# A gated linear recurrence: the factor of its input as (1 + a) times a root of tanh of half the exponent

## The chip, the core and the metric

The kernel runs on one core of one Trainium2 chip. The time is that of the device, in microseconds, from one execution's start to its end; a median is taken over executions of the same kernel. The engines are called by the profile's names: PE is TensorE's matmul, PEld its weight load, DVE is VectorE, ACT is ScalarE, POOL is GpSimd, SP is SyncE (which issues the DMAs).

## What is computed

Two layers over 512 tokens (256 of context, 256 latent) of width 2048. Each layer normalises and modulates its input, multiplies it with a large matrix `w_in`, feeds the columns to three mixers (a bidirectional gated linear recurrence, windowed attention, a bidirectional state-space part of the Mamba-2 kind), and multiplies the mix with `w_out`. The change concerns the recurrence, which runs in both directions over 1024 channels:

```python
r = sigmoid(einsum(xb, w_a) + b_a)             # 16 blocks of 64 x 64
i = sigmoid(einsum(xb, w_x) + b_x)
log_a = -LRU_C * r * softplus(-lam)            # LRU_C = 8
a = exp(log_a)
b = sqrt(-expm1(2.0 * log_a)) * (i * xf)
h = linear_scan(a, b, reverse)                 # h[t] = a[t] * h[t-1] + b[t]
```

The factor sqrt(1 - a^2) is what the two kernels write differently. With L = `log_a` and a = exp(L) both are exact:

- before: 1 - a^2 = -(1 + a^2) tanh(L), so the factor is the root of (1 + a^2) times -tanh(L);
- after: 1 - a = -(1 + a) tanh(L/2), so 1 - a^2 = -(1 + a)^2 tanh(L/2), and the factor is (1 + a) times the root of -tanh(L/2).

## The kernel before

Activations lie with channels on the partitions and tokens along the row (128x512 tiles, columns 0 to 255 context, 256 to 511 latent). The weights stay in float32 and come from HBM in pieces of 128x512, tile `raw`, on SP's DMA queue. Each piece becomes two matmul operands: `hi`, a rounded copy made on ACT (L237), and `lo`, the rest, a subtraction on DVE (L238), with four buffers each (`HB`). For every 128x128 block PE then runs three matmuls (`hi` with the input's `uh` and `ul`, `lo` with `uh`; L174) that add up in a PSUM tile `acc`. In the second layer the column blocks whose context half nobody reads (the recurrence's gate, among others) have 256 columns, not 512.

Around the change, a layer runs 8 blocks m of 128 channels: first the column block of the recurrence's input (`lru_x`), then that of its gate (`lru_g`). Between the weight matmuls PE runs small steps of the recurrence and of the state-space part, which share four PSUM tiles `mx`: for the recurrence the gate products (`mx<-xc,gw` and `mx<-xsw,gw`, for each direction d), for the state-space part steps of the classes State (tile `xw`, state `H`, L1119 to L1132) and Output (`cbm`, `ee`, `ww`, `bc`, L1151 to L1191). `xsw` (L694) is the convolved input `xc` with its two halves of partitions exchanged.

In `lru_x` each direction runs: two Tanh of the gate products on ACT (L712, into tiles `lt` for r and i), Tanh of the exponent into half of `ltl` (L717), Exp in place in `lt` (L718), Square into `la2` (L720), and on DVE (a^2 + 1) times tanh (L721) and (1 + tanh) times `xc` for the input gate (L722). When both directions are through, one Sqrt covers both halves of `ltl` (L724, 128x1024). It needs another table of functions in ACT than Tanh and Exp do, so an `ACT_TABLE_LOAD` stands ahead of it, and one ahead of the next Tanh or Exp. Then POOL multiplies the gated input with the root (L727), DVE scans (L730 forward; L733 and L735 backward in two halves), and POOL adds the directions (L739). `lru_g` (L745 to L750) multiplies this with the gate and stores it; the mix is read again at the layer's end.

What sets the order: PE's order is the program's own, written out by generators that wait for times in PE work by a table. The order on ACT, DVE, POOL and SP is made when the program is built, by a scheduler's own estimate of when each instruction can run; an engine then runs its list strictly in that order. The tile `la2` shares its four buffers with other roles (`xc`, `lgt`, `xw` among them). Line numbers here are those of the kernel before. In the changed kernel the first Tanh stands at L714, the Tanh of the exponent at L719 and Exp at L720; from L724 on the numbers are equal.

Of the kernel before, what the change touches and what calls it, by code (L numbers as in the profile page):

```python
# [10 lines left out]
AF = mybir.ActivationFunctionType  # L11
ALU = mybir.AluOpType
AX = mybir.AxisListType

P = 128
# [124 lines left out]
class Kernel:  # L140
# [526 lines left out]
    def lru_begin(self, l):  # L667
        nc = self.nc
        o = PARAMS["lam"][0]
        ng = self.t([P, 16], "nlam", 1)  # L670
        nc.vector.tensor_scalar(out=ng, in0=self.prm[:, o:o + 16], scalar1=-1.0, scalar2=None, op0=ALU.mult)
        sp = self.softplus(ng, 16, "lsp")
        self.s4 = self.t([P, 16], "s4", 1)
        nc.vector.tensor_scalar(out=self.s4, in0=sp, scalar1=-4.0, scalar2=None, op0=ALU.mult)
        self.gb = self.t([P, 32], "gbh", 1)
        o = PARAMS["gab"][0]
        nc.vector.tensor_scalar(out=self.gb, in0=self.prm[:, o:o + 32], scalar1=0.5, scalar2=None, op0=ALU.mult)
        self.gws = [self.gate_weights(l, 0)]
        self.lruD = self.dram([8, P, 512], "lruD")
# [8 lines left out]
    def lru_x(self, l, m, px):  # L688
        nc = self.nc
        xc = self.t([P, 512], "xc")  # L690
        self.conv(xc, px, lambda tap: self.par("lcw", tap * 8 + m), self.par("lcb", m), 2)
        xs = self.t([P, 512], "xsw")
        for r, o in ((0, 64), (64, 0)):
            nc.scalar.activation(out=xs[r:r + 64], in_=xc[o:o + 64], func=AF.Copy)  # L694
        gw = self.gws.pop(0)
        if m < 7:
            self.gws.append(self.gate_weights(l, m + 1))
        yield self.wait("lx")
        ab = []
        tl = self.t([P, 2, 512], "ltl", 1)  # L700
        for d in range(2):
            if d:
                yield self.wait("lx2")
            th = []
            pg = [self.mx() for _ in range(2)]
            for r, c in ((0, 0), (64, 64), (0, 64), (64, 0)):
                x = xc if r == c else xs
                self.mm(pg[r // 64][c:c + 64], gw[r:r + 64, int(r != c), 2 * d + r // 64], x[r:r + 64], pos=(r, c),
                        side=4)
            for g in range(2):  # L710
                t = self.t([P, 512], f"lt{g}", 2)
                nc.scalar.activation(out=t, in_=pg[g], func=AF.Tanh, scale=0.5,  # L712
                                     bias=self.gb[:, 16 * g + 8 * d + m:16 * g + 8 * d + m + 1])
                th.append(t)  # L714
            tr, ti = th
            s4 = self.s4[:, 8 * d + m:8 * d + m + 1]
            nc.scalar.activation(out=tl[:, d], in_=tr, func=AF.Tanh, scale=s4, bias=s4)  # L717
            nc.scalar.activation(out=tr, in_=tr, func=AF.Exp, scale=s4, bias=s4)  # L718
            a2 = self.t([P, 512], "la2", 1)  # L719
            nc.scalar.activation(out=a2, in_=tr, func=AF.Square)  # L720
            nc.vector.scalar_tensor_tensor(out=tl[:, d], in0=a2, scalar=1.0, in1=tl[:, d], op0=ALU.add, op1=ALU.mult)  # L721
            nc.vector.scalar_tensor_tensor(out=ti, in0=ti, scalar=1.0, in1=xc, op0=ALU.add, op1=ALU.mult)  # L722
            ab.append((tr, ti))
        nc.scalar.activation(out=tl, in_=tl, func=AF.Sqrt, scale=-0.0625, bias=self.eps["s"])  # L724
        hs = []
        for d, (tr, ti) in enumerate(ab):
            nc.gpsimd.tensor_tensor(out=ti, in0=ti, in1=tl[:, d], op=ALU.mult)  # L727
            h = self.t([P, 512], f"lh{d}", 2)
            if d == 0:
                nc.vector.tensor_tensor_scan(out=h, data0=tr, data1=ti, initial=0.0, op0=ALU.mult, op1=ALU.add)  # L730
            else:
                r = lambda x, s: x[:, s:s + 256][:, ::-1]
                nc.vector.tensor_tensor_scan(out=r(h, 0), data0=r(tr, 0), data1=r(ti, 0), initial=0.0, op0=ALU.mult,  # L733
                                             op1=ALU.add)
                nc.vector.tensor_tensor_scan(out=r(h, C), data0=r(tr, C), data1=r(ti, C), initial=h[:, 0:1],  # L735
                                             op0=ALU.mult, op1=ALU.add)
            hs.append(h)
        s = C if l else 0
        nc.gpsimd.tensor_tensor(out=hs[0][:, s:], in0=hs[0][:, s:], in1=hs[1][:, s:], op=ALU.add)  # L739
        self.lru_h[m] = hs[0]  # L740
# [536 lines left out]
```

## Time and profile before

| | |
|---|---|
| median of three runs | 1831.15 us (1829.35 to 1833.1) |
| profiled execution | 1829.47 us, its span 1827.5 us |
| mean granted clock of PE | 0.991 |
| PE busy | 1765.5 us, 97%, 10522 instructions |
| DVE busy | 1407.4 us, 77%, 3117 |
| ACT busy | 973.3 us, 53%, 1798 |
| POOL busy | 214.7 us, 12%, 179 |

The busy share is over the whole span; matmuls are pipelined, so a busy PE isn't PE at its peak. PEclk is the clock that was granted to PE as a share of full speed (1.0 is 2.4 GHz, 0.5 is 1.2 GHz). The two stages in which recurrence and state-space part run among the weight matmuls are 236 to 490 us (layer 0) and 1290 to 1500 us (layer 1); the profile can be asked for each stretch and for each engine's waits in it. In a list of waits an entry "PE mx L174 <- DVE H L1132" says that a matmul of PE into `mx` waited, and that the instruction that released it was DVE's on tile `H`, line 1132.

### The profile page before, as it was taken

How to read it: one execution, taken by the hardware profiler on the slowest of the kernel's cores; microseconds unless marked ns; L12 is line 12 of the kernel's file. 1: busy time of each engine (PE TensorE's matmuls, PEld its weight loads, DVE VectorE, ACT ScalarE, POOL GpSimd, SP SyncE). 2: the span in 40 equal slices, each digit the busy share in tenths (PEclk: the TensorE clock that was granted, in tenths of full speed). 3: DMA queues.
4: the chain of work that ended last, by engine and by line, in shares of the span. 5: the costliest groups of instructions: out<-in, count | busy, mean ns of one | idle time of the engine just before them, and what ended most of it. 6: DMA issues, size and time to landing. Idle time of an engine off the chain costs nothing.

```text
span 1827.5 us, 30170 instructions
## 1 busy us (share of the span) xinstructions
PE 1765.5 (97%) x10522; PEld 1453.4 (80%) x10522; DVE 1407.4 (77%) x3117; ACT 973.3 (53%) x1798; POOL 214.7 (12%) x179
## 2 busy tenths in 40 slices
PE   7999999999999999999999999999989999999999
PEld 4677876667778778887888887888767788999999
DVE  4447769898899778899999536877688785788665
ACT  4324578688523354556232235545688863678443
POOL 0000111111210021211000021010021130121000
PEclk9999999999999999999999999999999999999999
DMA  9982333434675545556766433455243564554655
GB/s 364 389 292 66 124 104 102 122 122 146 220 221 180 179 150 185 178 182 221 238 220 222 158 122 107 133 185 168 96 138 107 179 214 142 182 178 155 217 185 179
DMA packets 186344, 322.99 MB, mean 177 GB/s; under 512 B 19121, under 2 KB 44625, under 8 KB 185553
## 3 DMA queue, kind: packets, MB, share of 16 engines
q1 hardware_dynamic: 186192, 321.09, 54.2%
q8 instruction: 82, 1.34, 0.3%
q14 instruction: 70, 0.57, 0.1%
HBM read 310.38 MB, written 10.63 MB: 176 GB/s over the span
## 4 chain that ended last, share of the span: by engine, by line
PE 72%; DVE 9%; issue 7%; ACT 7%; DMA 3%; POOL 1%; SPq 0%; ACTq 0%; DVEq 0%; POOLq 0%
PE acc L174 55%; PE mx L174 13%; PE ada L174 3%; DVE lo L238 2%; PE mx L170 2%; DMA bc<-acsD 1%; ACT hi L237 1%; DVE ada L380 1%; DVE araw L380 1%; ACT lt L712 1%; DVE lh L730 1%; DMA araw<-in_adaw_dram 1%; DVE xc L466 1%; DVE ee L1165 1%; ACT ww L1167 1%
## 5 line engine op out<-in xcount | busy, mean ns | idle before, releaser
L174 PE MATMUL acc<-u,hi 128*128 128x512 f32 (+1 forms) x4800 | 1277.4, 355 | 3.9 <-ACT u L452 3.1
L174 PEld LDWEIGHTS acc<-u,hi 128*128 128x128 f32 x4800 | 837.1, 190 | 149.0 <-issue 32.6
L174 PE MATMUL acc<-u,lo 128*128 128x512 f32 (+1 forms) x2400 | 842.4, 351 | 6.9 <-DVE lo L238 6.7
L237 ACT ACTIVATE hi<-raw 128x512 fp32r<-128x512 f32 x640 | 397.8, 628 | 544.4 <-PE acc L174 420.8
L238 DVE TENSOR_TENSOR lo<-raw,hi 128x512 fp32r<-128x512 f32 x640 | 457.9, 718 | 184.6 <-ACT hi L237 172.7
L174 PEld LDWEIGHTS acc<-u,lo 128*128 128x128 f32 x2400 | 455.5, 190 | 71.9 <-DVE lo L238 11.7
L380 DVE SCALAR_TENSOR_TENSOR araw<-araw,adac 128x512 f32<-128x512 f32 x256 | 183.2, 716 | 6.9 <-DMA araw<-in_adaw_dram 4.1
L380 DVE SCALAR_TENSOR_TENSOR ada<-araw,adac 128x512 f32<-128x512 f32 x192 | 141.6, 738 | 13.0 <-DMA adac<-condD 7.0
L174 PE MATMUL mx<-u,hi 128*128 128x512 f32 (+1 forms) x320 | 99.7, 395 | 0.0
L1077 DVE SCALAR_TENSOR_TENSOR X<-acc,mod,X 128x256 f32<-128x256 f32 x144 | 65.0, 478 | 39.5 <-PE acc L174 39.4
L727 POOL TENSOR_TENSOR lt<-lt,ltl 128x512 f32<-128x512 f32 x32 | 45.5, 1443 | 326.2 <-ACT ltl L724 305.3
L868 POOL TENSOR_SCALAR prob<-prob,qrs 128x512 f32<-128x512 f32 (+1 forms) x48 | 58.2, 1227 | 214.7 <-ACT hi L237 124.7
L427 POOL TENSOR_TENSOR ssq<-ssq,sq 128x512 f32<-128x512 f32 (+1 forms) x26 | 34.1, 1312 | 308.0 <-ACT sq L423 308.0
L174 PEld LDWEIGHTS mx<-u,hi 128*128 128x128 f32 x320 | 56.6, 191 | 14.2 <-issue 4.6
L174 PE MATMUL mx<-u,lo 128*128 128x512 f32 (+1 forms) x160 | 61.0, 382 | 0.0
L511 POOL TENSOR_SCALAR X<-xs,prm 128x512 f32<-128x512 f32 (+1 forms) x16 | 15.4, 968 | 361.6 <-DVE xs L489 357.1
L174 PE MATMUL mx<-xc,gw 64*64 64x512 f32 x128 | 40.8, 619 | 8.9 <-ACT lt L712 5.9
L423 ACT ACTIVATE sq<-X 128x256 f32<-128x256 f32 (+1 forms) x44 | 18.8, 452 | 54.8 <-DVE X L654 53.1
L1165 DVE SCALAR_TENSOR_TENSOR ee<-bc,nacs,ee 128x128 f32<-128x128 f32 x96 | 35.9, 427 | 15.0 <-DMA bc<-acsD 9.6
L771 POOL TENSOR_TENSOR qw<-qw,cst 128x256 f32<-128x256 f32 x20 | 23.1, 1156 | 197.7 <-DVE rt L770 169.7
L712 ACT ACTIVATE lt<-mx,gbh 128x512 f32<-128x512 f32 x64 | 42.0, 674 | 4.1 <-PE mx L174 4.0
L1164 ACT ACTIVATE ee<-bc,nacs 128x128 f32<-128x128 f32 x96 | 30.9, 390 | 17.7 <-DMA bc<-acsD 17.7
(240 smaller groups left out, 1953.1 us busy)
## 6 DMA issues: line engine op xcount, KB each, us to landing
raw<-in_w_in_dram SPq DMA_DIRECT2D x448, 256.0 KB, 2.8
araw<-in_adaw_dram SPq DMA_DIRECT2D x256, 256.0 KB, 3.0
raw<-in_w_out_dram SPq DMA_DIRECT2D x192, 256.0 KB, 3.0
ar<-in_ada_dram SPq DMA_DIRECT2D x84, 256.0 KB, 5.4
bc<-acsD SPq DMA_DIRECT2D x48, 256.0 KB, 3.7
ar<-in_ada_dram SPq DMA_DIRECT2D x22, 512.0 KB, 6.9
adac<-condD SPq DMA_DIRECT2D x28, 256.0 KB, 4.5
gw<-in_gates_dram SPq DMA_DIRECT2D x16, 256.0 KB, 2.9
```

What stands on the lines that cost most here:

```text
L170: self.nc.tensor.transpose(out=out, in_=lhsT, identity=rhs)
L174: self.nc.tensor.matmul(out=out, lhsT=lhsT, rhs=rhs, start=start, stop=stop, **kw)
L237: nc.scalar.activation(out=hi, in_=part, func=AF.Copy)
L238: nc.vector.tensor_tensor(out=lo, in0=part, in1=hi.bitcast(F32), op=ALU.subtract)
L380: i = nc.vector.scalar_tensor_tensor(out=o, in0=raw, scalar=1.0, in1=row[c].rearrange("p t x -> p (t x)"), op0=ALU.mult, op1=ALU.mult, acc ...
L427: nc.gpsimd.tensor_tensor(out=self.ssq[0], in0=self.ssq[0], in1=sq, op=ALU.add)
L712: nc.scalar.activation(out=t, in_=pg[g], func=AF.Tanh, scale=0.5, bias=self.gb[:, 16 * g + 8 * d + m:16 * g + 8 * d + m + 1])
L727: nc.gpsimd.tensor_tensor(out=ti, in0=ti, in1=tl[:, d], op=ALU.mult)
L868: nc.gpsimd.tensor_scalar(out=pr[j], in0=pr[j], scalar1=rs[:, j:j + 1], scalar2=1.0, op0=ALU.mult, op1=ALU.mult)
L1077: nc.vector.scalar_tensor_tensor(out=x[:, s], in0=acc[:, s.start - w0:s.stop - w0], scalar=mod[:, 2 * KT + m, c:c + 1], in1=x[:, s], op0=A ...
L1164: nc.scalar.activation(out=e[:, j], in_=bcs[0][:, j], func=AF.Identity, bias=k.nacs[:, f:f + 1])
L1165: nc.vector.scalar_tensor_tensor(out=e[:, j], in0=bcs[1][:, j], scalar=k.nacs[:, r:r + 1], in1=e[:, j], op0=ALU.add, op1=ALU.min)
```

## The change

`lru_begin` gets a second constant, `s2` = -2 softplus beside `s4` = -4 softplus (a multiply of 128x16 per layer). In `lru_x` the Tanh of the exponent takes `s2`, so half the exponent. The Square, its tile `la2` and the product (a^2 + 1) times tanh go; the gated input, (1 + tanh) times `xc`, is multiplied by (1 + a) on DVE instead. Sqrt, POOL's products and the scans read as before.

```diff
--- before.py
+++ after.py
@@ -672,6 +672,8 @@
         sp = self.softplus(ng, 16, "lsp")
         self.s4 = self.t([P, 16], "s4", 1)
         nc.vector.tensor_scalar(out=self.s4, in0=sp, scalar1=-4.0, scalar2=None, op0=ALU.mult)
+        self.s2 = self.t([P, 16], "s2", 1)
+        nc.vector.tensor_scalar(out=self.s2, in0=sp, scalar1=-2.0, scalar2=None, op0=ALU.mult)
         self.gb = self.t([P, 32], "gbh", 1)
         o = PARAMS["gab"][0]
         nc.vector.tensor_scalar(out=self.gb, in0=self.prm[:, o:o + 32], scalar1=0.5, scalar2=None, op0=ALU.mult)
@@ -713,13 +715,11 @@
                                      bias=self.gb[:, 16 * g + 8 * d + m:16 * g + 8 * d + m + 1])
                 th.append(t)
             tr, ti = th
-            s4 = self.s4[:, 8 * d + m:8 * d + m + 1]
-            nc.scalar.activation(out=tl[:, d], in_=tr, func=AF.Tanh, scale=s4, bias=s4)
+            s4, s2 = (x[:, 8 * d + m:8 * d + m + 1] for x in (self.s4, self.s2))
+            nc.scalar.activation(out=tl[:, d], in_=tr, func=AF.Tanh, scale=s2, bias=s2)
             nc.scalar.activation(out=tr, in_=tr, func=AF.Exp, scale=s4, bias=s4)
-            a2 = self.t([P, 512], "la2", 1)
-            nc.scalar.activation(out=a2, in_=tr, func=AF.Square)
-            nc.vector.scalar_tensor_tensor(out=tl[:, d], in0=a2, scalar=1.0, in1=tl[:, d], op0=ALU.add, op1=ALU.mult)
             nc.vector.scalar_tensor_tensor(out=ti, in0=ti, scalar=1.0, in1=xc, op0=ALU.add, op1=ALU.mult)
+            nc.vector.scalar_tensor_tensor(out=ti, in0=tr, scalar=1.0, in1=ti, op0=ALU.add, op1=ALU.mult)
             ab.append((tr, ti))
         nc.scalar.activation(out=tl, in_=tl, func=AF.Sqrt, scale=-0.0625, bias=self.eps["s"])
         hs = []
```

Each of these edits stands 32 times in the program (2 layers, 8 blocks, 2 directions). PE's list is the same row by row in both kernels (8788 rows). ACT's goes from 1554 rows to 1523, DVE's from 2344 to 2345, and both have 69 `ACT_TABLE_LOAD`. All rows that differ in place lie in the two stages named above. Three places show how they do.

ACT, layer 1, second block (m = 1): from the second direction's Tanh (L712 before, L714 after) over the root (L724) to the next pieces of weights. `mx` is the gate product, `s` the exponent's factor, `gbh` the gate's bias, `xc<-acc` the convolution of the next block. Before:

```order
L712 ACTIVATE lt_2899_12991<-mx_12984,gbh_11799 128x512
L717 ACTIVATE ltl_12960<-lt_2898_12989,s_2638_11797 128x512
L237 ACTIVATE hi_13113<-raw_13111 128x512
L718 ACTIVATE lt_2898_12989<-lt_2898_12989,s_2638_11797 128x512
L720 ACTIVATE la_2900_12995<-lt_2898_12989 128x512
L460 ACTIVATE xc_13046<-acc_12858,prm_1005 128x512
L237 ACTIVATE hi_13151<-raw_13149 128x512
L237 ACTIVATE hi_13169<-raw_13167 128x512
L724 ACT_TABLE_LOAD
L724 ACTIVATE ltl_12960<-ltl_12960,epss_92 128x1024
L237 ACTIVATE hi_13235<-raw_13233 128x512
```

After:

```order
L719 ACTIVATE ltl_12928<-lt_2881_12955,s_2624_11769 128x512
L714 ACTIVATE lt_2882_12957<-mx_12950,gbh_11771 128x512
L720 ACTIVATE lt_2881_12955<-lt_2881_12955,s_2623_11767 128x512
L724 ACT_TABLE_LOAD
L724 ACTIVATE ltl_12928<-ltl_12928,epss_92 128x1024
L237 ACTIVATE hi_13077<-raw_13075 128x512
L460 ACTIVATE xc_13010<-acc_12826,prm_1005 128x512
L237 ACTIVATE hi_13115<-raw_13113 128x512
L237 ACTIVATE hi_13133<-raw_13131 128x512
```

The table load and the root now come directly behind the last Exp (L720 of after). A piece `hi` that stood between Tanh and Exp, the convolution and two more `hi` stood ahead of the load before, and stand behind the root now.

DVE, layer 0, sixth block (m = 5): a stretch that ends with the state `H` (L1132) for which PE waits. `bc` is a decay row times `CT`, `lh` a scan's output. Before:

```order
L238 TENSOR_TENSOR lo_4096<-raw_4093,hi_4095 128x512
L1176 TENSOR_TENSOR bc_4207<-bc_4207,CT_1802 128x512
L238 TENSOR_TENSOR lo_4196<-raw_4193,hi_4195 128x512
L735 SCALAR_TENSOR_TENSOR lh_800_3877<-lt_796_3862,lh_800_3877,lt_797_3864 128x256
L1132 TENSOR_TENSOR H_3657<-mx_4059,H_3657 128x512
L1119 TENSOR_TENSOR xw_4063<-X_1804,wst_2360 128x512
L1176 TENSOR_TENSOR bc_4209<-bc_4209,CT_1802 128x512
L238 TENSOR_TENSOR lo_4247<-raw_4244,hi_4246 128x512
L1130 TENSOR_TENSOR H_4204<-H_3657,dec_2358 128x512
L238 TENSOR_TENSOR lo_4281<-raw_4278,hi_4280 128x512
L1132 TENSOR_TENSOR H_3726<-mx_4102,H_3726 128x512
```

After:

```order
L1119 TENSOR_TENSOR xw_4045<-X_1804,wst_2362 128x512
L466 SCALAR_TENSOR_TENSOR xc_3970<-acc_3767,prm_172,xc_3970 128x2x255
L238 TENSOR_TENSOR lo_4174<-raw_4171,hi_4173 128x512
L1132 TENSOR_TENSOR H_3643<-mx_4041,H_3643 128x512
L1176 TENSOR_TENSOR bc_4187<-bc_4187,CT_1802 128x512
L238 TENSOR_TENSOR lo_4225<-raw_4222,hi_4224 128x512
L1130 TENSOR_TENSOR H_4182<-H_3643,dec_2360 128x512
L238 TENSOR_TENSOR lo_4259<-raw_4256,hi_4258 128x512
L746 SCALAR_TENSOR_TENSOR lgt_4071<-lgt_4071,acc_3980 128x512
L1132 TENSOR_TENSOR H_3712<-mx_4084,H_3712 128x512
```

The backward scan (L735) and one `bc` product have left the stretch ahead of this `H`; the convolution (L466) and the gate's product (L746) stand in it.

DVE, layer 0, second block (m = 1): the first Output of the state-space part, up to its product `ee` (L1171). Before:

```order
L1151 TENSOR_TENSOR cbm_2885<-mx_2881,cst_76 128x128
L1165 SCALAR_TENSOR_TENSOR ee_2891<-bc_2889,nacs_2356,ee_2891 128x128 x4
L721 SCALAR_TENSOR_TENSOR ltl_2809<-la_594_2844,ltl_2809 128x512
L1168 SCALAR_TENSOR_TENSOR ww_2892<-cbm_2885,dt_2151,ww_2892 128x128 x4
L1168 SCALAR_TENSOR_TENSOR ww_2955<-cbm_2885,dt_2151,ww_2955 128x128 x4
L1176 TENSOR_TENSOR bc_2887<-bc_2887,CT_1802 128x512
L238 TENSOR_TENSOR lo_3038<-raw_3035,hi_3037 128x512
L1191 TENSOR_TENSOR X_1805<-mx_2940,X_1805 128x2x128
L1171 TENSOR_TENSOR ee_2891<-ee_2891,ww_2892 128x512
```

After:

```order
L1151 TENSOR_TENSOR cbm_2879<-mx_2875,cst_76 128x128
L1165 SCALAR_TENSOR_TENSOR ee_2885<-bc_2883,nacs_2358,ee_2885 128x128 x4
L730 SCALAR_TENSOR_TENSOR lh_592_2844<-lt_586_2814,lt_587_2816 128x512
L1168 SCALAR_TENSOR_TENSOR ww_2886<-cbm_2879,dt_2153,ww_2886 128x128 x4
L733 SCALAR_TENSOR_TENSOR lh_593_2847<-lt_590_2834,lt_591_2836 128x256
L1168 SCALAR_TENSOR_TENSOR ww_2949<-cbm_2879,dt_2153,ww_2949 128x128 x4
L735 SCALAR_TENSOR_TENSOR lh_593_2847<-lt_590_2834,lh_593_2847,lt_591_2836 128x256
L238 TENSOR_TENSOR lo_3032<-raw_3029,hi_3031 128x512
L1176 TENSOR_TENSOR bc_2881<-bc_2881,CT_1802 128x512
L1191 TENSOR_TENSOR X_1805<-mx_2934,X_1805 128x2x128
L1130 TENSOR_TENSOR H_2779<-H_2779,dec_2360 128x512
L1171 TENSOR_TENSOR ee_2885<-ee_2885,ww_2886 128x512
```

The product of L721 is gone; the three scans of the block (L730, L733, L735) and a step of the state `H` (L1130) now stand ahead of `ee`.

## Rows read from the trace of the kernel before

**Rows 1.** Busy us by stage: start:end length, then each engine (count), PEclk, DMA.

```profile
236.00:490.00 254.00, 240.61 (x1248) 174.80 (x1247) 214.09 (x421) 192.98 (x361) 41.53 (x30) 0.97 0.41 132
...
1290.00:1500.00 210.00, 195.49 (x1284) 153.59 (x1277) 174.44 (x306) 168.99 (x297) 43.50 (x36) 0.99 0.46 144
```

**Rows 2.** Whom PE waited for, 236 to 490: us in total, times, longest.

```profile
PE mx L174 <- DVE ee L1171: 4.5, 2, 3.1
PE mx L174 <- ACT lt L712: 3.1, 1, 3.1
PE mx L174 <- DVE H L1132: 2.7, 1, 2.7
PE mx L174 <- ACT xsw L694: 2.3, 1, 2.3
```

**Rows 3.** The same for 1290 to 1500.

```profile
PE mx L174 <- ACT lt L712: 9.7, 7, 4.1
PE acc L174 <- DVE lo L238: 4.7, 5, 1.6
```

**Rows 4.** Groups by line and form: count | busy us, mean ns | idle before.

```profile
L238 DVE TENSOR_TENSOR lo<-raw,hi 128x512 fp32r<-128x512 f32 x640 | 457.9, 718 | 184.6 <-ACT hi L237 172.7 <-DMA ar<-in_ada_dram 5.5 <-PE acc L174 2.0
...
L730 DVE TENSOR_TENSOR_SCAN lh<-lt,lt 128x512 f32<-128x512 f32 x16 | 29.0, 1813 | 8.9 <-POOL lt L727 8.9
...
L722 DVE SCALAR_TENSOR_TENSOR lt<-lt,xc 128x512 f32<-128x512 f32 x32 | 22.1, 689 | 21.5 <-ACT lt L712 21.3
L721 DVE SCALAR_TENSOR_TENSOR ltl<-la,ltl 128x512 f32<-128x512 f32 x32 | 21.9, 687 | 5.2 <-ACT la L720 5.0
...
L720 ACT ACTIVATE la<-lt 128x512 f32<-128x512 f32 x32 | 20.0, 628 | 0.6
```

**Rows 5.** Timeline of ACT, layer 1, second block: start us, us, engine, instruction.

```profile
1320.21 0.62 ACT L237 ACTIVATE hi<-raw 128x512 fp32r<-128x512 f32 x1
1320.73 0.81 ACT L718 ACTIVATE lt<-lt,s 128x512 f32<-128x512 f32 x1
1321.57 0.63 ACT L720 ACTIVATE la<-lt 128x512 f32<-128x512 f32 x1
1322.11 0.76 ACT L460 ACTIVATE xc<-acc,prm 128x512 f32<-128x512 f32 x1
1322.77 1.14 ACT L237 ACTIVATE hi<-raw 128x512 fp32r<-128x512 f32 x2
1323.93 1.28 ACT L724 ACT_TABLE_LOAD   x1
1325.22 1.15 ACT L724 ACTIVATE ltl<-ltl,epss 128x1024 f32<-128x1024 f32 x1
1326.28 1.13 ACT L237 ACTIVATE hi<-raw 128x512 fp32r<-128x512 f32 x2
```

**Rows 6.** Timeline of DVE and PE, layer 0, sixth block; [idle before <- releaser].

```profile
403.26 0.74 DVE L735 TENSOR_TENSOR_SCAN lh<-lt,lh,lt 128x256 f32<-128x256 f32 x1
...
405.82 1.77 DVE L1176 TENSOR_TENSOR bc<-bc,CT 128x512 f32<-128x512 f32 x1
...
409.32 0.68 DVE L1132 TENSOR_TENSOR H<-mx,H 128x512 f32<-128x512 f32 x1
...
410.05 0.65 PE L174 MATMUL mx<-xc,gw 64*64 64x512 f32 x2 [2.75 <-DVE H L1132]
```

**Rows 7.** The same, layer 0, second block; last row as rows 1.

```profile
281.44 0.68 DVE L1171 TENSOR_TENSOR ee<-ee,ww 128x512 f32<-128x512 f32 x1
...
283.89 0.45 PE L174 MATMUL mx<-ee,X 128*64 128x128 f32 x4
...
293.20 0.70 PE L174 MATMUL mx<-ee,X 128*64 128x128 f32 x4 [3.15 <-DVE ee L1171]
...
291.00:296.00 5.00, 2.80 (x18) 2.40 (x19) 5.00 (x8) 2.08 (x5) 2.12 (x2) 0.64 0.42 146
```

**Rows 8.** Pieces of weights on ACT and their matmuls on PE, layer 1.

```profile
1321.57 0.40 PE L174 MATMUL acc<-u,hi 128*128 128x256 f32 x2
...
1476.66 0.62 ACT L237 ACTIVATE hi<-raw 128x512 fp32r<-128x512 f32 x1
...
1478.22 0.40 PE L174 MATMUL acc<-u,hi 128*128 128x256 f32 x2
```

**Rows 9.** Timeline of ACT and PE ahead of the longest wait of layer 1.

```profile
1338.69 2.44 ACT L1167 ACTIVATE ww<-cbm,dt 128x128 f32<-128x128 f32 x8 [1.97 <-DVE cbm L1151]
...
1341.67 1.29 ACT L1164 ACTIVATE ee<-bc,nacs 128x128 f32<-128x128 f32 x4 [0.54 <-DMA bc<-acsD]
...
1344.11 1.22 PE L174 MATMUL mx<-xw,Btok 128*128 128x512 f32 x1 [4.12 <-ACT lt L712]
```

## The prediction

> **What bounds the kernel now.** I read the busy time by stage first. Both recurrence stages are TensorE-paced but not TensorE-full: in 236 to 490 us (layer 0) PE is busy 240.61 of 254.00 us, in 1290 to 1500 us (layer 1) 195.49 of 210.00; ACT has 192.98 and 168.99 there, DVE 214.09 and 174.44 [rows 1]. So ACT is busy 76% and 80% of the two stages, DVE 84% and 83%, and PE idles 13.4 and 14.5 us. These 27.9 us, and what the clock loses behind them, are all that the change can win, because the orders of the two kernels differ only inside these stages, and PE's own order is the same row by row.
>
> Next I read whom PE waits for. In layer 0 the named waits are DVE's `ee` 4.5 us (longest 3.1), ACT's `lt` 3.1, DVE's `H` 2.7 and ACT's `xsw` 2.3 [rows 2]. None is a wait for weights (`hi`, `lo`); all come from the `mx` banks that the recurrence and the state-space part share. In layer 1 it is `lt` 9.7 us in seven waits (longest 4.1) and `lo` 4.7 in five [rows 3]. The reader is to see that `Square` and the product that are removed stand in none of these rows by name: they act only by standing in a queue ahead of something that does.
>
> **The change part by part.** Each of 16 blocks (8 per layer) handles two directions, so every edit counts 32.
>
> Removed from ACT: 32 Square at 628 ns mean, 20.0 us busy in all [rows 4]. In a full queue one costs less than its length: from the start of one to the next instruction is 1322.11 - 1321.57 = 0.54 us [rows 5]. That is 17 us of queue room, some 1.1 us per block of 25 to 30 us.
>
> DVE: 32 products `ltl` go (21.9 us, 687 ns), 32 products (1 + a) times the gated input come. The added form (scalar and tensor, 128x512, both inputs in SBUF) is that of L722, 689 ns [rows 4]. 32 x (689 - 687) is nothing. Two multiplies of 128x16 for the new constant, one per layer ahead of its recurrence, I price at zero, since DVE has idle time there; the bound is one L722 each, 1.4 us, if they stood on the path. POOL's two products, the scans and the number of table loads are unchanged.
>
> Moved: `Sqrt` needed Exp, Square and the DVE product. Now it needs only the two Tanh. In layer 1's second block the last Exp starts at 1320.73 and Sqrt at 1325.22, 4.49 us later [rows 5]; in the new order Exp is followed at once by the load and Sqrt, which is 0.84 (Exp to the next) + 1.29 (load to Sqrt) = 2.13 us. So the recurrence's chain (Sqrt, POOL's products, scans) starts about 2.4 us earlier from there, more where two Squares stood ahead. The scans have a fixed place in DVE's queue and move ahead of other work there. No consumer of the chain's end is near, since the mix of the recurrence is read at the end of the layer; what can win is what the scans used to stand in front of.
>
> Layer 0, wait by wait:
> - `H`, 2.75 us at 410.05. DVE's L1132 ran at 409.32 behind the last scan at 403.26 and a `bc` product of 1.77 us at 405.82 (this one and its neighbours are stretched beside POOL's products of the same block) [rows 6]. In the new order no scan stands in this stretch; one of 0.74 alone and the 1.1 us by which the 1.77 exceeds a usual 0.68 are 1.8, the two others (mean 1.81 and about 0.7) bring it over 2.75. I take -2.8; bounds 0 and -2.8, since more than the wait can't be won.
> - `ee`, 3.15 us at 293.20. Here the scans leave the second Output's stretch and enter the first one's. Its `ee` product ran at 281.44 to 282.12 and PE took it at 283.89, so 1.8 us of slack [rows 7]. Ahead of it come scans of 1.81, about 0.7 and 0.74, less the removed product of 0.69: 2.6, and a `lo` or two of 0.72. A new wait of 1 to 2.5 us at 283.89 is thus likely, and the later one shrinks by as much or more. I take 0, bounds +2 and -5.0: the 3.15, and 1.8 us more of clock. In 291 to 296 us, behind that gap, the granted clock was 0.64 (part of it at 1.2 GHz, the rest at 2.4) [rows 7]; (1 - 0.64) x 5 = 1.8 us is what that window gives back if the gap goes.
> - `xsw`, 2.3: the new order puts `xsw` ahead of eight `ww`, but the `ee` that follows on PE then waits for these `ww`. I take -0.5, bounds 0 and -2.3.
> - `lt`, 3.1: one more ACT instruction (`lgt`) now stands ahead of it; +0.5 by the step of 0.54 [rows 5], bounds 0 and +0.6.
> Sum of layer 0: -2.8.
>
> Layer 1. Here matmuls have 256 columns in half of the blocks, and a piece of weights is used up twice as fast, so `hi` is late by little. **The cost of the change is here**: load and Sqrt used to stand behind two or three `hi`, and now stand ahead of them. In the second block `hi` was at 1320.21, right behind `ltl`; now Exp (0.84), the load (1.29) and Sqrt (1326.28 - 1325.22 = 1.06) come first, and one Square (0.54) less: 3.19 - 0.54 = 2.65 us later [rows 5]. The slack was 1321.57 - (1320.21 + 0.62) = 0.74 [rows 8], so PE waits 1.9. In the order I find five such places in eight blocks; in the last, Exp stood ahead already, so 1.29 + 1.06 - 0.54 = 1.8 later against a slack of 1478.22 - (1476.66 + 0.62) = 0.94: 0.9 [rows 8]. I take 1.2 for each of the five, +6.0; bounds 0 (the queue ahead runs so early that each fits) and 5 x 2.65 = +13.3.
>
> On the price of the load: the row has it at 1323.93 for 1.28, the two pieces ahead of it start at 1322.77 and take 1.14 together, so end at 1323.91, and Sqrt starts 1.29 after the load does [rows 5]. The Trainium skill (ScalarE: Activation LUTs, What ACT_TABLE_LOAD costs) counts, besides a load of about 1283 ns, a drain of about 1380 ns ahead of it, 2.66 us for each switch. These rows leave no room for such a drain; with it the five places would, as an estimate from that section, cost 6.9 us more.
>
> Against it stand two gains. Of the 9.7 us of `lt` the longest, 4.1 before 1344.11, hangs on eight `ww` (2.44 us, late by 1.97) and on an `ee` that waited 0.54 for a DMA [rows 9], all of which stay in place; the other 5.6 come partly from a queue that starts with the convolution behind the scans. I take a quarter of the whole, -2.5, bounds 0 and -5.6. Of the 4.7 us of `lo`, some goes with the Squares and with scans that run before, I take a third, -1.5, bounds 0 and -4.7.
> Sum of layer 1: 6.0 - 2.5 - 1.5 = +2.0.
>
> All: -2.8 + 2.0 = -0.8 us against the profiled execution's 1829.47 us (span 1827.5 and 2.0 around it): 1828.7. That execution stands 1.7 us under the median, so the forecast is 1831.15 - 0.8 = 1830.3.
>
> **The rivals.**
> (A) Faster: the moved scans clear the shared `mx` banks in layer 0, -2.8 (`H`), -5.0 (`ee` with its clock), -1.5 (`xsw`), and layer 1's `lt` gives -5.6 while the weights cost +6.0: -8.9, 1822. For it: in layer 0 the slack of `hi` and `lo` is several us, so ACT's lump costs nothing. Against it: in the first Output's stretch the scans are now in the way.
> (B) Slower: load plus Sqrt in one lump ahead of the weights, in layer 1's 256-column blocks, at full price 5 x 2.65 = 13.3, against which only -2.8 and -2.5 stand: +8, 1839. It decides from the point where a `hi` behind the lump has under 2.65 us of slack; two places shown have 0.74 and 0.94.
> (C) Slower because the load right behind Exp has to let ACT run empty, which the load behind `hi` pieces need not: priced at a second length of the load, 1.28 [rows 5], at five places 6.4: -0.8 + 6.4 = +5.6, 1837. The load shown starts 0.02 behind the end of the instruction ahead, so it has 0.02. The Trainium skill's section named above states such a drain; no load in these rows shows it.
> (D) The change doesn't do what it says for the time: ACT is off the path, Square was in its idle share, every wait finds another releaser: 0, 1831. It falls together with the forecast.
>
> **How the numbers follow.** A run of this kernel can be told from no change at about 0.2%, 3.7 us. Forecast with (D), within that: 0.38. (A) and smaller gains over 3.7 us: 0.36. (B) 0.24 and (C) 0.02: slower 0.26. The sum is close to zero because gains and costs of about 8 us each offset one another, so neither sign is excluded. The range goes from (A)'s 1822 a little below, for a part of `lo`, to (B): 1821 to 1839. The forecast's own range is 1827.5 to 1834.5.
>
> **What would show each step.** Right: ACT's busy time 20 us less; DVE's the same within 1; the last Exp to Sqrt about 2.1 us in most blocks; the 2.75 us wait for `H` gone; in layer 1 new waits of PE for `hi` or `lo` of 1 to 2 us just behind Sqrt, their total over 8 us; `lt` under 9.7. Wrong: if PE's idle time in 1290 to 1500 falls below 12 us, the lump is hidden and (A) holds; if layer 0 keeps over 13 us, the scans only moved the waits and (B) is near. A difference outside the two stages would break the premise that nothing else is touched.

## The result, and the profile after

The changed kernel takes 1841.65 us (median, 1839.92 to 1849.61) against 1831.15: a ratio of 1.0066, 95% interval 1.0048 to 1.0085. It is slower, by 12 us by the ratio (9 to 16 by its interval) and 10.5 by the medians, and 2.7 us outside the range that was given. The profiled execution took 1841.65 us, with a span of 1839.7. One execution of `square_kept` (2160 us) and one of the kernel before (3480 us) fell into a slower state and are left out of every median and ratio below.

The page of the changed kernel, engines' busy time:

```profile
span 1839.7 us, 30167 instructions
PE 1768.6 (96%) x10522; PEld 1454.3 (79%) x10522; DVE 1408.1 (77%) x3119; ACT 959.5 (52%) x1766; POOL 218.8 (12%) x179
```

ACT is busy 13.8 us less (its instructions take 20.2 us less in sum; the busy time counts overlaps once), and DVE is as busy as before. PE runs the same instructions, but takes 3.1 us longer for them; the other 9.1 of the 12.2 us by which the span grew are idle time of PE. Where it lies is seen by stage (columns as in rows 1; the stages end later than before, so both windows are a little longer than those of rows 1):

```profile
236.00:495.00 259.00, 241.65 (x1263) 174.77 (x1263) 216.29 (x426) 186.58 (x348) 48.67 (x32) 0.98 0.40 132
1290.00:1510.00 220.00, 200.30 (x1289) 155.80 (x1288) 175.52 (x306) 162.59 (x281) 43.95 (x36) 0.98 0.42 135
```

PE now idles 17.4 us in the first stage and 19.7 in the second; it was 13.4 and 14.5 in [rows 1]. Whom it waits for most, first from 236 to 495, then from 1300 to 1510:

```profile
PE mx L174 <- DVE ee L1171: 9.5, 3, 5.7
PE mx L174 <- ACT lt L714: 3.7, 1, 3.7
PE mx L174 <- DVE H L1132: 2.1, 2, 1.7
```

```profile
PE mx L174 <- ACT lt L714: 11.3, 5, 5.0
PE acc L174 <- ACT hi L237: 4.3, 4, 1.7
PE acc L174 <- DVE lo L238: 4.0, 5, 0.9
```

Against [rows 2] the wait for `ee` has doubled and `xsw` is gone; against [rows 3] there are four waits for `hi` that did not exist.

Since PE's order is the same row by row, each matmul of one kernel can be set beside the same matmul of the other. What a stage adds is how much further behind the kernel before its last matmul is than its first. This table, worked out from the traces, has all kernels of the study but `square_kept` (us, one profiled execution each, against the profile of before; stages from the matmul at 248.5 to that at 493.6 and from 1285.7 to 1499.9 us of before; "all" is the lag of the last matmul; "rest" is all else, where no edit stands and nearly all rows keep their order: the text ahead has all rows that moved inside the two stages, but in the traces some of ACT's and DVE's, up to 546 us, moved as well):

```
kernel                 layer 0  layer 1   rest    all
the change               +1.5     +7.1    +3.1   +11.8
the change, again        +4.3     +8.8    -1.2   +11.9
square_kept_look         +5.4    +15.2    +2.8   +23.3
no_square                +0.3     -5.3    -0.4    -5.4
late_root                +0.3     -4.0    +3.2    -0.5
layer1_only              -0.6     +6.7    +1.8    +7.9
root_late_in_layer1      +3.1     -3.1    +3.1    +3.1
no_load                  -6.5     -2.4    +3.1    -5.9
two_products             -3.5     -2.2    +1.7    -4.0
store_pool               +1.0     +9.1    +3.3   +13.5
mixed_root               -2.9     -2.9    +4.7    -1.2
mixed_root_store         -3.5     +0.9    +2.4    -0.2
```

The "rest" runs from -1.2 to +4.7 for rows that no edit touches: that is the scatter of single profiles, that of before included, which at 1829.47 us is 1.7 us or more under the medians of this kernel. A difference of under 3 us in one cell is read only where the medians agree.

What a stage adds is not idle time alone. Layer 1's stage from its first to its last matmul, so the same 1302 matmuls, for the kernel before, the change, the change again and `layer1_only`; the last row is a stretch of the change:

```profile
1285.67:1499.95 214.28, 199.77 (x1302) 156.75 (x1300) 176.38 (x309) 170.19 (x299) 43.50 (x36) 0.99 0.45 142
1290.23:1511.65 221.42, 201.72 (x1302) 157.26 (x1301) 176.44 (x307) 163.07 (x281) 43.95 (x36) 0.98 0.42 136
1288.43:1511.54 223.11, 203.84 (x1302) 159.85 (x1301) 176.02 (x307) 163.66 (x282) 43.67 (x36) 0.97 0.44 136
1287.00:1507.94 220.94, 204.50 (x1302) 159.12 (x1301) 176.07 (x307) 163.03 (x281) 45.26 (x36) 0.96 0.45 136
1375.95:1382.78 6.83, 4.33 (x8) 2.81 (x9) 5.17 (x10) 6.80 (x13) 0.00 (x0) 0.50 0.12 41
```

PE is idle 14.5, 19.7, 19.3 and 16.4 us of them, so the change adds 5.2 and 4.8 us of waits; and it is busy 2.0, 4.1 and 4.7 us longer than before with the same matmuls. The granted clock goes with that: in this stage it was 0.5 (1.2 GHz) for 3.4 us before, and for 10.2, 13.7 and 17.1 us in the three others, each time around waits of PE (the stretch in the last row begins inside the wait of 5.05 us that ends at 1378.45). In layer 0 the change adds 4.0 and 4.3 us of idle time in its two profiles; that the stage came out as +1.5 and +4.3 is a difference in PE's busy time. So the waits repeat better than the lengths. No run sets the clock apart from the waits that it follows.

**Layer 1, the second block.** The timeline of the changed kernel, ACT, POOL, DVE and PE, over the stretch that [rows 5] and [rows 8] show of the kernel before:

```profile
1324.57 0.80 ACT L720 ACTIVATE lt<-lt,s 128x512 f32<-128x512 f32 x1
...
1325.39 1.28 ACT L724 ACT_TABLE_LOAD   x1
...
1326.69 1.15 ACT L724 ACTIVATE ltl<-ltl,epss 128x1024 f32<-128x1024 f32 x1
1327.74 0.61 ACT L237 ACTIVATE hi<-raw 128x512 fp32r<-128x512 f32 x1
...
1327.91 2.96 POOL L727 TENSOR_TENSOR lt<-lt,ltl 128x512 f32<-128x512 f32 x2 [10.71 <-ACT ltl L724]
...
1328.39 1.34 DVE L238 TENSOR_TENSOR lo<-raw,hi 128x512 fp32r<-128x512 f32 x1 [1.79 <-ACT hi L237]
1328.41 0.50 PE L174 MATMUL acc<-u,hi 128*128 128x256 f32 x2 [1.74 <-ACT hi L237]
...
1329.79 0.39 PE L174 MATMUL acc<-u,lo 128*128 128x256 f32 x1 [0.88 <-DVE lo L238]
```

Exp, the load and Sqrt stand one behind the other for 3.2 us. The piece `hi` behind them ends at 1328.35, and PE, which asks for it 1.74 us earlier, stands. Then it stands again for the `lo` of the same piece, which DVE can only make from `hi`, and which takes 1.34 us and not 0.69, while POOL's products (1327.91 to 1330.87) run beside it. The same pair of waits comes three times more, in the last three blocks:

```profile
1443.21 0.73 PE L174 MATMUL acc<-u,hi 128*128 128x512 f32 x2 [1.02 <-ACT hi L237]
1444.60 0.50 PE L174 MATMUL acc<-u,lo 128*128 128x512 f32 x1 [0.66 <-DVE lo L238]
...
1467.93 0.50 PE L174 MATMUL acc<-u,hi 128*128 128x256 f32 x2 [0.70 <-ACT hi L237]
1469.31 0.39 PE L174 MATMUL acc<-u,lo 128*128 128x256 f32 x1 [0.88 <-DVE lo L238]
...
1491.79 0.50 PE L174 MATMUL acc<-u,hi 128*128 128x256 f32 x2 [0.81 <-ACT hi L237]
1493.17 0.39 PE L174 MATMUL acc<-u,lo 128*128 128x256 f32 x1 [0.88 <-DVE lo L238]
```

Matmul against matmul the four places cost 1.90, 1.18, 0.86 and 0.97 us for `hi` and 1.03, 0.82, 1.04 and 1.04 for `lo`: 8.8 us. At all four POOL's products (L727) have started about 0.5 us ahead of the `lo`, and the `lo` takes 1.34 to 1.36 us. That is 2.7 us more than four of 0.69, and the four waits for `lo` are 3.3 us together: most of this second wait goes with POOL, whose products the early root set off.

**Layer 0, the second block**, ACT, DVE and PE of the changed kernel, where [rows 7] show that PE took `ee` at 283.89 with 1.8 us to spare:

```profile
275.81 1.28 ACT L724 ACT_TABLE_LOAD   x1
...
277.11 1.15 ACT L724 ACTIVATE ltl<-ltl,epss 128x1024 f32<-128x1024 f32 x1
...
278.59 3.00 DVE L1165 SCALAR_TENSOR_TENSOR ee<-bc,nacs,ee 128x128 f32<-128x128 f32 x4 [1.36 <-ACT ee L1164]
279.34 2.44 ACT L1167 ACTIVATE ww<-cbm,dt 128x128 f32<-128x128 f32 x8
...
282.31 1.28 ACT L1175 ACT_TABLE_LOAD   x1
...
284.14 0.62 ACT L1170 ACTIVATE ee<-ee 128x512 f32<-128x512 f32 x1
...
288.84 1.75 DVE L1171 TENSOR_TENSOR ee<-ee,ww 128x512 f32<-128x512 f32 x1
...
290.73 0.70 PE L174 MATMUL mx<-ee,X 128*64 128x128 f32 x4 [5.75 <-DVE ee L1171]
```

Load and Sqrt come before the first Output's `ee` and `ww`, so the load that brings Exp's table back falls into the Output too (282.31). Its Exp ends at 284.76, when PE is about to ask (290.73 - 5.75 = 284.98). Then DVE has the last scan, a `lo`, a `bc` product, a step of `X` and one of `H` ahead of the product: it comes at 288.84, and takes 1.75 us beside POOL, which is at work from 286.13 on.

### The profile page after: what moved, and what is told of

Its sections match the earlier page's. It is cut to its first block, busy times and chain, and to the rows that moved or that the text cites. A ratio compares the mean times of both kernels' runs of the same rounds, so it can differ in the third digit from the quotient of the medians.

```text
span 1839.7 us, 30167 instructions
## 1 busy us (share of the span) xinstructions
PE 1768.6 (96%) x10522; PEld 1454.3 (79%) x10522; DVE 1408.1 (77%) x3119; ACT 959.5 (52%) x1766; POOL 218.8 (12%) x179
## 3 DMA queue, kind: packets, MB, share of 16 engines
q8 instruction: 82, 1.34, 0.3%
## 5 line engine op out<-in xcount | busy, mean ns | idle before, releaser
L238 DVE TENSOR_TENSOR lo<-raw,hi 128x512 fp32r<-128x512 f32 x640 | 465.5, 730 | 190.5 <-ACT hi L237 179.1
L727 POOL TENSOR_TENSOR lt<-lt,ltl 128x512 f32<-128x512 f32 x32 | 45.8, 1454 | 312.7 <-ACT ltl L724 312.7
L1165 DVE SCALAR_TENSOR_TENSOR ee<-bc,nacs,ee 128x128 f32<-128x128 f32 x96 | 31.0, 375 | 27.0 <-DMA bc<-acsD 20.2
L714 ACT ACTIVATE lt<-mx,gbh 128x512 f32<-128x512 f32 x64 | 42.2, 674 | 10.8 <-PE mx L174 10.8
```

What stands on the lines that cost most here:

```text
L238: nc.vector.tensor_tensor(out=lo, in0=part, in1=hi.bitcast(F32), op=ALU.subtract)
L1165: nc.vector.scalar_tensor_tensor(out=e[:, j], in0=bcs[1][:, j], scalar=k.nacs[:, r:r + 1], in1=e[:, j], op0=ALU.add, op1=ALU.min)
```

## The experiments

**Theory 1**, formed on this profile: what costs the time is the place of the table load and Sqrt, right behind Exp and ahead of weights and of `ee`; the removed Squares are a gain. **Theory 2**: PE's waiting times are set by hand to fit the order of before, so that any shift of ACT and DVE costs some 10 us. First the changed kernel again, with three kernels that share the runs of before (median 1832.43).

**The change again** (no edit).

> The changed kernel itself, unchanged, as the yardstick of this group. Both theories: 1838 to 1845 us against a kernel before of 1829 to 1833. Where its matmuls lag behind those of the kernel before should repeat: about +1 us over layer 0's recurrence stage, +7 us over layer 1's; what the first profile showed outside of them (+0.9 in the first 33 us, +2.6 between 495 and 1290), where both kernels run the same order, should come out different if it is scatter, and the same if it belongs to the change.

Measured: 1841.97 us (1838.25 to 1846.21), ratio 1.0051, 95% interval 1.0037 to 1.0066. In both stages the idle time of PE repeats (4.3 and 4.8 us more than before, where it was 4.0 and 5.2), the lag less well (table), and the rest came out as -1.2 where it was +3.1. So that part is scatter.

**Square and the place of the root, one at a time.** Three edits; `late_root` and `square_kept` start from the changed kernel, `no_square` from the kernel before:

```diff
 late_root
-        nc.scalar.activation(out=tl, in_=tl, func=AF.Sqrt, scale=-0.0625, bias=self.eps["s"])
+        late = self.t([P, 1], "late", 2)
+        nc.vector.tensor_scalar(out=late, in0=ab[1][1][:, 0:1], scalar1=0.0, scalar2=2e-35, op0=ALU.mult, op1=ALU.add)
+        nc.scalar.activation(out=tl, in_=tl, func=AF.Sqrt, scale=-0.0625, bias=late)
 no_square
-            a2 = self.t([P, 512], "la2", 1)
-            nc.scalar.activation(out=a2, in_=tr, func=AF.Square)
-            nc.vector.scalar_tensor_tensor(out=tl[:, d], in0=a2, ...
+            nc.vector.scalar_tensor_tensor(out=tl[:, d], in0=tr, ...
 square_kept
+            a2 = self.t([P, 512], "la2", 1)
+            nc.scalar.activation(out=a2, in_=tr, func=AF.Square)
```

> The changed formula, but Sqrt's bias is a small tile (128x1) that DVE makes from the product (1 + a) times the gated input, so that table load and Sqrt can't start before Exp and that product are through; in the order they fall behind two to five pieces of weights again. Theory 1 (the place of table load and Sqrt, right behind Exp and ahead of the weights, is the whole cost): layer 1's waits for hi vanish, its stage is within 2 us of the kernel before, the first Output of layer 0 loses its 5.8 us wait, total 1827 to 1834. Theory 2 (the hand-set waiting times fit the order of before, and any shift of ACT and DVE costs some 10 us): 1838 to 1845, with waits at other places.

> The kernel before without its 32 Squares: the product takes a where it took a squared, so the recurrence's factor is another number; all else, Sqrt's dependence on that product too, is as before. It removes the 20 us of ACT and nothing else. Theory 1: the root keeps its late place, so 1826 to 1833, a gain of 0 to 4 us. Theory 2: 1838 to 1845.

> The changed kernel with the 32 Squares computed into a tile that nobody reads: ACT's work is as before, but Sqrt still needs only the two Tanh. In the order the load and Sqrt stand right behind Exp, the Squares behind them. Theory 1: as slow as the changed kernel or more, 1840 to 1850, with hi waits of 1 to 2 us behind Sqrt in layer 1. A third theory (the Squares were a spacing that kept the weights in step): 1829 to 1834. Theory 2 gives 1838 to 1845 too.

Measured: `late_root` 1828.73 us, ratio 0.9976 (0.9964 to 0.9988); `no_square` 1827.16, 0.9966 (0.9953 to 0.9979); `square_kept` 1848.8, 1.0086 (1.0072 to 1.0101). The first of them is the change with nothing but the root held back, by a small tile: 1841.97 - 1828.73 = 13.2 us. The two others make a table of two by two, with the kernel before and the change in the corners top left and bottom right. Its two columns also differ in where DVE multiplies: under the root on the left, on the gated input on the right.

```
                      root late    root early    early costs
Squares there          1832.4        1848.8         16.4
Squares gone           1827.2        1842.0         14.8
removal gains             5.3           6.9
```

Theory 2 falls: two other orders of ACT and DVE are faster than the one that the waiting times were set for. Theory 1 holds on both its halves: the place of the root, with all that follows it, costs 13 to 16 us, and the Squares are worth some 5 to 7. The idea that Squares were a useful spacing falls too. In the traces nothing stands between the last Exp and the load in any of the change's 16 blocks; in layer 1 of `late_root` two to four pieces of weights do. ACT's timeline of `late_root` in layer 1's second block shows what the held root does:

```profile
1321.37 0.80 ACT L720 ACTIVATE lt<-lt,s 128x512 f32<-128x512 f32 x1
1322.07 0.61 ACT L237 ACTIVATE hi<-raw 128x512 fp32r<-128x512 f32 x1
1322.59 0.76 ACT L460 ACTIVATE xc<-acc,prm 128x512 f32<-128x512 f32 x1
1323.26 1.14 ACT L237 ACTIVATE hi<-raw 128x512 fp32r<-128x512 f32 x2
1324.41 1.28 ACT L726 ACT_TABLE_LOAD   x1
1325.71 1.15 ACT L726 ACTIVATE ltl<-ltl,late 128x1024 f32<-128x1024 f32 x1
```

Three pieces of weights stand ahead of the load again, and the waits of PE in that stage (1290 to 1510) have no `hi` left:

```profile
PE mx L174 <- ACT lt L714: 8.8, 4, 3.4
PE acc L174 <- DVE lo L238: 3.4, 5, 0.9
```

For the waits of the kernel with dead Squares one more execution was profiled; it has no interval:

> The changed kernel with its dead Squares once more, for its waits, since it was timed without a profile that can be used. With load and Sqrt right behind Exp: hi waits in layer 1 of 4 us or more in sum, lo waits of 3 or more behind them, and its layer 1 stage 7 to 14 us behind the kernel before. If the Squares cost something elsewhere: hi waits under 4 and the loss in layer 0's ee, H or lt.

It took 1852.99 us; PE's longest waits from 1290 to 1512:

```profile
PE acc L174 <- DVE lo L238: 9.0, 9, 1.8
PE acc L174 <- ACT hi L237: 6.9, 5, 2.1
PE mx L174 <- ACT lt L714: 4.9, 3, 2.3
```

As theory 1 has it: more work on ACT behind the early root makes the same two waits longer, 6.9 for `hi` and 9.0 for `lo`. The stage is 15.2 us behind the kernel before, a little more than expected.

**Which layer, and the load itself** (the kernel before at 1831.9 in this group). `layer1_only` puts the change under `if l == 1`; `root_late_in_layer1` is `late_root` with the small tile in layer 1 only; `no_load` replaces `AF.Sqrt` by `AF.Identity` in the changed kernel.

> The change in layer 1 alone; layer 0 is as in the kernel before. From the two profiles of the changed kernel, layer 1's stage costs +7.1 and +8.8 us, layer 0's +1.5 and +4.3. If the two layers' costs are separate: 1838 to 1842 against a kernel before of 1832, so most of the loss. If layer 0's disorder matters later: under 1836.

> The changed formula in both layers, with the root held behind the product in layer 1 alone; in layer 0 the root keeps its early place. Layer 1's stage should be some 4 us faster than in the kernel before, as with the root late in both; layer 0's should cost +1.5 to +4.3 as in the changed kernel: 1829 to 1834, that is 1 to 4 us above the kernel with the late root in both layers. If the early place is harmless in layer 0 (the forecast's view of it): 1825 to 1828.5.

> The changed kernel with Sqrt replaced by an Identity of the same tile and shape, which leaves the root out: the recurrence's factor is another number. It needs no other table, so 32 of 69 table loads go; the instruction stands at the same early place, ahead of the same pieces of weights. Theory 1a (the load in that place is the cost): the four hi waits of 1.7, 1.2, 0.9 and 1.0 in layer 1 shrink by 1.28 each to under 1 in sum, the lo waits behind them as well, layer 0's ee wait of 5.8 to about 3: 10 to 16 us less than the changed kernel, 1826 to 1832. Theory 1b (the cost is that POOL's products and the scans run early and stand before other work, whatever the load): 1838 to 1845.

Measured: `layer1_only` 1838.02 us, 1.0037 (1.0025 to 1.0050); `root_late_in_layer1` 1831.4, 0.9998 (0.9985 to 1.0011); `no_load` 1823.07, 0.9953 (0.9939 to 0.9968). So layer 1 carries most of the loss (6 us, 7 in its stage). Not all of that goes through `hi`: in `layer1_only` PE waits for it only twice in layer 1 (1290 to 1510),

```profile
PE acc L174 <- ACT hi L237: 1.4, 2, 0.7
```

and of the 6.7 us 1.9 are idle time and 4.7 longer matmuls (rows above). The early root in layer 0 alone costs 0.0022 of the time against `late_root`, 4 us, with intervals that overlap a little; PE's waits for `ee` are there as in the change (longest 5.7 us, 2.1 in `late_root`). So it is likely not harmless. And the early place without the load is not only harmless: it is 9 us faster than the kernel before and 18 faster than the change by the ratios, more than theory 1a had expected. By the traces ACT, DVE and POOL run the same rows in the same order as in the change, with Identity at the very place of Sqrt and 37 loads for 69. PE's waits of `no_load` in layer 1 (1290 to 1510):

```profile
PE mx L174 <- ACT lt L714: 8.1, 5, 3.4
PE acc L174 <- DVE lo L238: 2.6, 4, 0.9
PE acc L174 <- ACT hi L237: 0.6, 2, 0.3
```

The `hi` waits went from 4.3 to 0.6 us. This speaks for the load and against theory 1b: POOL's products and the scans stand as early here, and only the loads are gone. But it takes away 32 loads, those that bring the Exp table back too, 32 x 1.28 = 41 us of ACT, so it doesn't price the 16 in front of Sqrt alone.

**Later still.** `two_products` keeps the (1 + a) under the root, squared, with two DVE products and no product on the gated input:

```diff
-            nc.vector.scalar_tensor_tensor(out=ti, in0=tr, scalar=1.0, in1=ti, op0=ALU.add, op1=ALU.mult)
+            for _ in range(2):
+                nc.vector.scalar_tensor_tensor(out=tl[:, d], in0=tr, scalar=1.0, in1=tl[:, d], op0=ALU.add, op1=ALU.mult)
```

> The same factor with the (1 + a) inside the root: DVE multiplies tanh of half the exponent twice by (1 + a), Sqrt covers both halves as before, no Square, no product on the gated input. Against the late root of the changed formula it has 31 more DVE products of 0.69 (21 us) and a root that is later by one of them. If ACT's queue is what matters and DVE has room: within 3 us of the late root, 1826 to 1832. If DVE, busy 84% of the stages, is short: 1833 to 1845 with more waits for lo, ee and H.

Measured: 1824.78 us, 0.9963 (0.9951 to 0.9975). It computes the same factor, and beats both kernels; it is 1.2 us below the range expected for it, and 2.4 us faster than `late_root` by the ratios, with intervals that overlap. Its root is late again: in layer 1 two to four pieces of weights stand between the last Exp and it. 21 us more of DVE cost nothing that can be seen; DVE's room was not what bound the stage.

**One wait of layer 1 that theory 1 had not explained**: at block m = 2 PE waited 5.05 us for `lt`, before 1.27. The kernel before at 1834.84 in this group. `store_pool` is the changed kernel with `nc.gpsimd.dma_start` in place of `nc.sync.dma_start` for the stores of `lruD`; `mixed_root` takes layer 0 from `two_products` and layer 1 from `late_root`; `mixed_root_store` has both edits.

> The changed kernel with one edit: the 16 stores of the recurrence's result (lruD) are issued by POOL, right behind its own product, and no longer by SP. The order of ACT is the same row by row. Open is why PE's wait for lt at block m = 2 of layer 1 grew from 1.3 to 5.1 us: on SP's list the store stands ahead of two loads of decay rows (bc) there in the changed kernel, behind them in the kernel before. If the store holds bc up: that wait falls by 2 to 4 us, 1836 to 1840 against the changed kernel's 1842. If it is the pieces of weights ahead of bc, which wait for lo: no change, 1840 to 1844. If an issue from POOL is dear for POOL: slower than 1842.

> Layer 0 as in the kernel with two products under the root, layer 1 with the late root of the changed formula. By the profiles layer 0's stage was -3.5 us in the one, layer 1's -4.0 in the other, against the kernel before. If the two add: 1822 to 1826 against a before of 1832. If those differences are scatter of single profiles: 1825 to 1829, as each of the two.

> The kernel with a root late in both layers (two products in layer 0, the changed formula in layer 1) and the stores of the recurrence's result issued by POOL. There the stores stand behind the decay rows on SP's list, so if the theory of the store is right it brings little: within 2 us of the same kernel without it.

Measured: `store_pool` 1844.22 us, 1.0049 (1.0036 to 1.0061); `mixed_root` 1827.81, 0.9962 (0.9949 to 0.9976); `mixed_root_store` 1829.35, 0.9972 (0.9961 to 0.9983). My theory of the store fell. Without the store on its list SP issues the decay rows as late as in the changed kernel, and PE waits no less (`store_pool`, SP's issues, ACT and PE):

```profile
1370.05 0.92 SPq L1158 DMA_DIRECT2D bc<-acsD  x2
1374.63 1.28 ACT L1164 ACTIVATE ee<-bc,nacs 128x128 f32<-128x128 f32 x4 [5.03 <-DMA bc<-acsD]
...
1378.78 2.08 PE L174 MATMUL mx<-xw,Btok 128*128 128x512 f32 x2 [5.63 <-ACT lt L714]
```

What is ahead of the `bc` loads on SP's list is a piece of weights whose buffer comes free with a `lo` of DVE; in the changed kernel these rows show it:

```profile
1368.65 1.23 DVE L238 TENSOR_TENSOR lo<-raw,hi 128x512 fp32r<-128x512 f32 x1
...
1369.91 0.33 SPq L234 DMA_DIRECT2D raw<-in_w_in_dram  x1
1370.33 0.87 SPq L1158 DMA_DIRECT2D bc<-acsD  x2
```

The `lo` ends at 1369.88, the piece is issued 0.03 later, `bc` behind it. A scan that stands ahead of this `lo` now, and stood behind it before, is the likely cause of the lateness; that was only read from the two timelines. That the chain starts at the early load would fit `no_load` and `late_root`, where the longest `lt` wait is 3.4; but `square_kept_look` has the early load too, and its longest is 2.3. No run took away this scan alone, and this stays open. `mixed_root` is as fast as `two_products` by ratio, not faster: the gains of the two do not add to anything that these runs can tell.

## Why the prediction was wrong

It named the mechanism, load and Sqrt as one lump ahead of operands that PE needs, and most of the places; the sum failed, and the likeliest case was not the one that came. Layer 0 was put at -2.8 us and came out at +1.5 and +4.3 in the two profiles of the change, layer 1 at +2.0 and came out at +7.1 and +8.8. Four steps failed: the gain at `H`, the gain at `lt` in layer 1, the lump's second wait (`lo`), and PE's longer matmuls in layer 1, which are in no term.

- **The lump in layer 1** (taken as 1.2 at five places, +6.0). Right for what it counted: 1.9 was worked out for the second block and 0.9 for the last, 1.90 and 0.97 were measured, and the four places that came cost 4.9 for `hi`. What was left out is the `lo` of the same piece. It hangs on the `hi` by DVE, and took twice its usual time beside POOL's products, which follow the early root; so every late `hi` made PE wait a second time, 3.9 us in all; 8.8 in place of 6.0. The slack of `hi` alone was read, not the chain `hi`, `lo`, matmul behind it.
- **The `lt` gain in layer 1** (taken as -2.5). The wait at 1344.11 shrank, 2.9 us with the matmuls behind it, and that at m = 2 grew by 3.8, 4.8 with those behind it: +2.0, and 11.3 for 9.7 in the list of waits. The bounds, 0 and -5.6, allowed for no loss, although the instructions that move ahead of these waits were known. This is the term with the wrong sign.
- **The `lo` gain** (taken as -1.5, bound -4.7). The five old waits of [rows 3] went wholly, 5.5 us by the matmuls: they lie behind places where PE now stands anyway. Their size was lost to the new ones: 4.0 in the list.
- **PE's own time in layer 1** (in no term). The same matmuls took 2.0 and 4.1 us longer in the two profiles, with 10.2 and 13.7 us at 1.2 GHz for 3.4. Some of it is counted above already, as matmuls behind a wait. The prediction priced the clock once, for the gap at `ee` in layer 0.
- **`ee` in layer 0** (taken as 0, bound +2). The new wait at 283.89 was put at 1 to 2.5 us; it is 5.8. The sum had only DVE's scans in it. Load and Sqrt ahead of `ee` and `ww` on ACT (2.4 us), the second load (1.3) and DVE's work stretched beside POOL (2.9 us in the two rows shown) were not in it. The first scan it put at the mean of 1.81, where it took 1.21, so that step was rather too dear. The later wait of 3.15 did go, so that the block costs about 1 net by 305 us.
- **`H` in layer 0** (taken as -2.8). The wait at 410.05 fell from 2.75 to 0.39, but PE got there no earlier: against the kernel before it was 4.28 us behind at 391.38 and 3.93 at 410.05, so 0.35 was won. PE had lost 2.1 us more at the gate products from 404.22 to 405.13, where it had not waited before; and `H` itself made PE wait anew at another place (1.68 us where the kernel before is at 320.20). The order shown ahead of the prediction has the convolution and the gate's product in this stretch; the prediction gave them no price.
- **`xsw`** (taken as -0.5): 2.5 us won at 441.06 and 2.6 lost at the `ee` right behind it, as the text had it.
- **The Squares** were priced only through these waits. By `no_square` they are worth 5.3 us by the medians and 6.2 by the ratio (3.8 to 8.6 by its interval), most of it in layer 1 by its one profile. In the sum they are hidden behind the loss.

Of the rivals, (B), slower by the lump, has the sign and the cause that came. That its 1839 is only 3 us short is luck: it took 13.3 us for waits on `hi` where 4.9 came, and set gains of 2.8 and 2.5 against them where the one was 0.35 and the other a loss; `lo`, `ee` and PE's longer matmuls made up the difference. Its 0.24 was too little: its price stood on rows, the gains set against it on what might go. (C), the load with a drain, did not come: see the last section. The range ended at (B) with no room for a loss in layer 0, though the prediction itself called a new wait at `ee` likely.

## What to carry to other kernels

Removing an instruction also removes a wait, and the scheduler will run what waited at the first moment it can: look where a long lump (here load and Sqrt, 2.4 us) goes in a strict queue, and what with little slack falls behind it. If the early place hurts, a false dependency (here a 128x1 tile) puts it back and keeps the gain: 0.9976 in place of 1.0051 against the same runs of before. When a late `hi` is priced, follow it through every engine to the next matmul: here the `lo` behind it made PE wait a second time, since the early root had also brought POOL's products beside it. And when two profiles are compared, set PE's idle time and its busy time beside each other for the same matmuls: here the idle time repeated and the busy time moved by some us.

## What the runs showed of the hardware

A table load costs its own 1.28 us and little more, also right behind an instruction of the other table. All 69 loads in the trace of the change take 1.283 us, and 68 of them start within 0.02 us of the end of the instruction ahead. In the rows of layer 1's second block Exp starts at 1324.57 and takes 0.80, the load starts at 1325.39, 0.02 after Exp's end, and Sqrt 1.30 after the load. The little more is an overlap: two ACTIVATEs in a row overlap by some 0.1 us (in `late_root` one starts at 1322.07, takes 0.61, and the next starts at 1322.59), a load does not. The Trainium skill (ScalarE: Activation LUTs, What ACT_TABLE_LOAD costs) adds a drain of about 1380 ns to each switch; the trace does not show one here.

DVE's operations on two tensors can take twice as long while POOL is at work: `lo` 1.34 us at 1328.39 where 0.69 is usual, four `ee` 3.00 for 1.13, one `ee` product 1.75 for 0.68. In the trace of the change the 17 `lo` that run mostly beside POOL's products (L727) take 1.34 to 1.82 us, and the 530 with no POOL beside them at most 0.70. The one that starts second has the longer time: the `lo` at 285.97 starts 0.16 us ahead of POOL's sum of the directions (L739) and takes 0.66, and this sum takes 2.24, where another takes 1.28. The Trainium skill (SBUF — State Buffer, SBUF: two separate sides) says that the two share a pair of ports and that the one that comes second is blocked for the other's whole instruction; the longer times, and which side has them, agree with that; no run was made to test it. At the four places of layer 1 this adds to the cost of the early root, since POOL's products start right behind it and run beside just the `lo` that PE waits for.
